# Mixer scan phase: weights split by a rounding load and an adding load, and high-half matmuls ahead of low-half ones

## The chip, the cores and the metric

The kernel runs on one core of one Trainium2 chip. The metric is the device time of one execution in microseconds (us); lower is better. A difference under about 0.2% cannot be told from none.

## What is computed

The reference is a stack of two blocks over 512 tokens of width 1024, batch 1, all in 32-bit floats. The first block has two layers, each a mixer and a feed-forward part; the second has one layer with another mixer and a two-matrix MLP. The change concerns the mixer of the first block:

```python
def _mixer(h, w_in, ...):
    p = h @ w_in                                  # 1024 x 6672
    (qkv, z, beta_r, a_r, hq, hf_fwd, hf_bwd, hi, hgate, gate_dn, gate_hg) = _split(p, IN_SIZES)
    ...                                           # 5-tap depthwise conv, silu, norms
    o_f = _gated_delta_rule(q, k, v, beta[0], g[0])          # 4 heads of 128, forward
    o_b = _flip(_gated_delta_rule(_flip(q), ...))            # and backward
    ...
    o_hf = _hgrn2_scan(qh, outs[0][0], ih, outs[0][1])       # 4 heads of 128, both directions
    ...
    merged = (jax.nn.sigmoid(gate_dn) * (o_dn @ w_branch_dn)
              + jax.nn.sigmoid(gate_hg) * (o_hg @ w_branch_hg))
    return merged @ w_out
```

## The kernel before

**Big products.** Every product with a weight matrix goes through `gemm` (line 264). A weight tile is 128 output columns by 8 blocks of 128 rows, 512 KB. `weights` (line 235) loads it from HBM into `wr` on SP's queue (line 244, three buffers), ScalarE (ACT) copies it to `wh`, rounded to the matmul's reduced 32-bit format fp32r (line 245, two buffers), and VectorE (DVE) subtracts, `wl = wr - wh`, which is what the rounding left over (line 246, two buffers). The moving operand is split the same way into `xh` and `xl`. For each of the 8 blocks `mm3` queues three matmuls into one PSUM bank `pd`: `wh` by `xh`, `wh` by `xl`, `wl` by `xh`, 24 for a tile, all recorded at line 257 (line 259 in a paced stretch).

**The scan phase of a mixer** runs twice, once for each layer, in the order of the string `ORDER`: four heads of the gated delta rule (`gdn_front`, `gdn_inverse`, `gdn_scan`) and four of the second scan (`hg_head`). It needs 37 weight tiles: a small one (`w_ba`, 16 columns) and 36 of 512 KB (nine for each head number: Q, K, V, Z of the first scan and two gates, query, input and output gate of the second). Beside these run chains of small steps: matmuls of 128x128 blocks, with DVE, ACT and GpSimd (POOL) working in turn between them. In `gdn_front`, `raw` (line 449) takes a product out of PSUM and DVE's line 454 makes the 5-tap convolution; `er` and `gb` are gate rows fetched by DMA; in `hg_head` each of seven steps has a copy `kc` on ACT (line 680), four matmuls (line 682), `att` and `qk` on DVE (lines 684, 686) and `pq` mostly on POOL (line 687).

**Order.** Each engine works through its own list in order, and an instruction that waits holds what is behind it. The lists are made when the program is built, by a scheduler that places instructions by priority and its own timing of them; the high-priority parts are those of the delta rule's chain. Weight loads are alone on SP's queue. POOL's queue before the change holds its elementwise steps and, outside the scan phases, eight small DMAs.

After a scan phase come gates, branch products and the output product, then the feed-forward part: long runs of weight tiles.

Of the kernel before, what the change touches and what calls it, by code (L numbers as in the profile page):

```python
# [173 lines left out]
class Net:  # L174
    def __init__(self, tc, I, O, at, ctx):
# [11 lines left out]
        self.n = 0  # L187
        self.pace, self.paced = [], 0
# [46 lines left out]
    def weights(self, src, lo="v", small=None):  # L235
        nc = self.nc
        n, c = src.shape[1], src.shape[2]
        pl, k, bf = (self.wp, 8, (3, 2, 2)) if small is None else (small, 2, (2, 2, 2))
        raw, hi, lw = (pl.tile([P, k, P], dt, name=self.nmx(t), tag=t, bufs=b) for t, dt, b in zip(("wr", "wh", "wl"), (F32, F32R, F32R), bf))
        if c == P:  # L240
            raw, hi, lw = raw[:, :n], hi[:, :n], lw[:, :n]
        else:
            raw, hi, lw = (t.rearrange("p a b -> p (a b)")[:, :n * c].rearrange("p (a b) -> p a b", b=c) for t in (raw, hi, lw))
        nc.sync.dma_start(raw, src)
        nc.scalar.activation(hi, raw, AF.Copy)  # L245
        (nc.vector if lo == "v" else nc.gpsimd).tensor_tensor(lw, raw, hi.bitcast(F32), op=ALU.subtract)  # L246
        return hi, lw
# [6 lines left out]
    def mm(self, *a, **k):  # L254
        """a matmul; those of a paced stretch are queued behind the steps of a scan, a few after each"""
# [8 lines left out]
    def gemm(self, srcs, xs, lo="v", m=P):  # L264
        bank = self.bank("pd")
        ps = bank[:m]
        nk = sum(s.shape[1] for s in srcs)
        k = 0
        for s in srcs:
            hi, lw = self.weights(s, lo)  # L270
            for i in range(s.shape[1]):
                self.mm3(ps, hi[:, i], lw[:, i], xs[k][0], xs[k][1], k == 0, k == nk - 1)
                k += 1
# [53 lines left out]
    def norm2_end(self, st):  # L327
        """the final norm of the first block and the first of the second in one"""
# [68 lines left out]
    def gdn_small(self, l, xs, rb, sp):  # L397
        """token-major gates of all heads: columns (c, d*4+h)"""
# [79 lines left out]
    def pair(t, width, b, first, off, n):  # L478
        """columns off .. off + n of a tile [P, 2 * width], blocks of b taken in turn from its halves, from half `first` at the start"""
# [238 lines left out]
    def mixer(self, l, state):  # L718
        nc, tc = self.nc, self.tc
        xs, rb = state  # L720
        with tc.tile_pool(name=f"sp{l}", bufs=1) as sp, tc.tile_pool(name=f"gt{l}", bufs=2) as gt:
            with tc.tile_pool(name=f"gi{l}", bufs=1) as self.gi, tc.tile_pool(name=f"gp{l}", bufs=1) as gp:
                with tc.high_priority():
# [6 lines left out]
                for u in ORDER.split():  # L730
# [8 lines left out]
                    else:  # L739
                        dn[h] = self.gdn_scan(l, h, xs, rb, sm, gp, sp, fr[h], zf[h])  # L740
                W = self.I[f"w_in{l}"]
# [478 lines left out]
```

## Time and profile before

| | |
|---|---|
| time, median of 3 runs | 2744.57 us (2740.33 to 2746.9) |
| span of the profiled execution, first to last instruction | 2742.3 us |
| TensorE (PE) busy | 2645.3 us, 96% |
| DVE busy | 1556.6 us, 57% |
| ACT busy | 1124.7 us, 41% |
| POOL busy | 329.2 us, 12% |

The page of the profile gives the span of its execution; which of the three times belongs to it is not listed, and between the span and the median lie 2.3 us. Busy time of PE is counted from modelled ends of matmuls, so it overlaps; idle time of PE and the clock that it was granted are the more useful columns.

### The profile page before, as it was taken

The page shows a single profiled execution, that of the slowest core. Times are in us where ns is not written, and L with a number is a line of the kernel's source. Part 1 is how long each engine was busy: PE and PEld are TensorE (multiplying, and loading weights), DVE is VectorE, ACT ScalarE, POOL GpSimd, SP SyncE. Part 2 cuts the span into 40 slices and gives each one's busy share as a digit, 9 for nine tenths or more (in the row PEclk, how much of TensorE's full clock was granted, in tenths as well). Part 3 has the DMA queues.
Part 4 walks back from the last instruction along what each step waited for, and adds up shares of the span by engine and source line. Part 5 has one row for each costly group of instructions (what it writes and reads, how often), then busy time and mean ns, then how long its engine had stood idle before and what let it go on. Part 6 is the DMA issues. An engine that isn't in the chain of part 4 may idle for free.

```text
span 2742.3 us, 32455 instructions
## 1 busy us (share of the span) xinstructions
PE 2645.3 (96%) x12674; PEld 2178.6 (79%) x12674; DVE 1556.6 (57%) x2234; ACT 1124.7 (41%) x1511; POOL 329.2 (12%) x282
## 2 busy tenths in 40 slices
PE   7999899999999979998999999999999999999999
PEld 4788788878888857887888788888777788888887
DVE  6778764455554366778644555534874444553442
ACT  6545544343333255455443433333446443332221
POOL 1112320001110011122200011100100111000000
PEclk9999989999999999999999999999999999999999
DMA  4112212253223332111123423234411232433332
GB/s 149 62 49 67 62 39 68 88 167 100 94 98 114 121 89 70 55 61 54 39 76 101 160 95 100 93 121 127 145 64 51 82 96 94 140 129 99 94 104 88
DMA packets 99064, 254.13 MB, mean 93 GB/s; under 512 B 10016, under 2 KB 31520, under 8 KB 98656
## 3 DMA queue, kind: packets, MB, share of 16 engines
q1 hardware_dynamic: 66960, 215.17, 24.5%
q10 hardware_dynamic: 31568, 35.85, 4.5%
q8 instruction: 100, 1.64, 0.2%
q0 software_dynamic: 384, 1.05, 0.1%
q14 instruction: 52, 0.43, 0.1%
HBM read 238.36 MB, written 12.62 MB: 92 GB/s over the span
## 4 chain that ended last, share of the span: by engine, by line
PE 49%; ACT 1%; DVE 0%; issue 0%; POOL 0%; ACTq 0%; DVEq 0%; POOLq 0%
PE pd L257 45%; PE ph L1065 1%; PE pl L1053 1%; PE pd L259 1%; ACT wh L245 0%; PE pr L1061 0%; ACT L1179 0%; PE pl L972 0%; PE ph L682 0%; PE pl L843 0%; DVE wl L246 0%; ACT rb L294 0%; ACT rb L295 0%; PE pl L1015 0%; PE ph L1039 0%
## 5 line engine op out<-in xcount | busy, mean ns | idle before, releaser
L257 PE MATMUL pd<-xh,wh 128*128 128x512 f32 (+1 forms) x3186 | 1265.8, 398 | 36.3 <-DVE raw L449 14.3
L257 PE MATMUL pd<-xh,wl 128*128 128x512 f32 (+1 forms) x3188 | 1258.0, 395 | 2.6 <-DVE wl L246 2.3
L257 PE MATMUL pd<-xl,wh 128*128 128x512 f32 (+1 forms) x3186 | 1253.7, 394 | 2.1 <-DVE xl L290 2.0
L245 ACT ACTIVATE wh<-wr 128x1024 fp32r<-128x1024 f32 (+5 forms) x449 | 434.9, 969 | 1011.3 <-PE pd L257 866.8
L257 PEld LDWEIGHTS pd<-xh,wh 128*128 128x128 f32 (+1 forms) x3186 | 600.2, 188 | 178.8 <-issue 20.9
L257 PEld LDWEIGHTS pd<-xl,wh 128*128 128x128 f32 (+1 forms) x3186 | 600.3, 188 | 139.2 <-issue 7.2
L257 PEld LDWEIGHTS pd<-xh,wl 128*128 128x128 f32 (+1 forms) x3188 | 600.0, 188 | 138.7 <-DVE wl L246 5.0
L246 DVE TENSOR_TENSOR wl<-wr,wh 128x1024 fp32r<-128x1024 f32 (+5 forms) x449 | 521.7, 1162 | 250.3 <-ACT wh L245 244.1
L1179 ACT ACT_TABLE_LOAD x116 | 148.8, 1283 | 8.7 <-issue 4.4
L394 DVE TENSOR_TENSOR g<-pd,rb 128x512 f32<-128x512 f32 x64 | 44.3, 692 | 158.2 <-PE pd L257 148.1
L803 POOL TENSOR_TENSOR fs<-fs,rb 128x512 f32<-128x512 f32 x44 | 56.9, 1294 | 506.3 <-ACT fs L802 506.3
L682 PE MATMUL ph<-pq,kc 128*128 128x128 f32 x448 | 74.8, 313 | 19.6 <-POOL er L569 6.7
L797 DVE TENSOR_TENSOR fg<-pd,rb 128x512 f32<-128x512 f32 x44 | 30.5, 693 | 109.9 <-PE pd L257 107.0
L682 PEld LDWEIGHTS ph<-pq,kc 128*128 128x128 f32 x448 | 66.7, 213 | 26.4 <-issue 19.2
L687 POOL TENSOR_TENSOR pq<-pq,f 128x512 f32<-128x512 f32 x48 | 58.8, 1225 | 230.7 <-PE ph L682 211.5
L805 DVE TENSOR_TENSOR fs<-fs,pd 128x512 f32<-128x512 f32 x44 | 30.3, 688 | 90.0 <-POOL fs L803 90.0
L801 DVE SCALAR_TENSOR_TENSOR fs<-fg,cv,fs 128x512 f32<-128x512 f32 x88 | 65.9, 749 | 3.6 <-ACT fs L799 1.9
L802 ACT ACTIVATE fs<-fs 128x512 f32<-128x512 f32 x44 | 27.8, 632 | 85.5 <-DVE fs L801 85.5
L394 DVE TENSOR_TENSOR mh<-pd,rb 128x512 f32<-128x512 f32 x32 | 22.1, 692 | 70.2 <-PE pd L257 68.8
L680 ACT COPY kc<-qk 128x512 f32<-128x512 f32 x56 | 36.9, 659 | 52.2 <-PE ph L682 44.5
L454 DVE SCALAR_TENSOR_TENSOR qk<-raw,cv,qk 128x512 f32<-128x512 f32 x64 | 54.1, 858 | 2.6 <-ACT qk L452 2.2
L684 DVE COPY_PREDICATED att<-um,ph 128x512 f32<-128x512 uint8 x56 | 41.2, 736 | 21.5 <-PE ph L682 21.2
(332 smaller groups left out, 2442.5 us busy)
## 6 DMA issues: line engine op xcount, KB each, us to landing
wr<-in_w_in_dram SPq DMA_DIRECT2D x126, 512.0 KB, 3.3
wr<-in_w_up_dram SPq DMA_DIRECT2D x88, 512.0 KB, 3.3
wr<-in_w_m_dram SPq DMA_DIRECT2D x64, 512.0 KB, 3.8
wr<-in_w_dn_dram SPq DMA_DIRECT2D x32, 512.0 KB, 3.6
wr<-in_w_gt_dram SPq DMA_DIRECT2D x32, 512.0 KB, 3.3
wr<-in_w_out_dram SPq DMA_DIRECT2D x24, 512.0 KB, 3.4
xd<-xn ACTq DMA_DIRECT2D x40, 256.0 KB, 2.0
xo<-xd ACTq DMA_DIRECT2D x32, 256.0 KB, 2.8
```

Source lines behind the costliest of these rows:

```text
L245: nc.scalar.activation(hi, raw, AF.Copy)
L246: (nc.vector if lo == "v" else nc.gpsimd).tensor_tensor(lw, raw, hi.bitcast(F32), op=ALU.subtract)
L257: return self.nc.tensor.matmul(*a, **k)
L394: self.nc.vector.tensor_tensor(out, ps, rb, op=ALU.mult)
L454: V.scalar_tensor_tensor(o, raw[:, j:j + T], self.col(f"dnc{l}_{j}", ch), o, op0=ALU.mult, op1=ALU.add)
L680: A.copy(kc.rearrange("p (n e b) -> p n e b", e=2, b=hh), self.pair(qk, T, hh, 0, 0, T))
L682: PE.matmul(pl[:, c], kc[:, c * P:(c + 1) * P], self.pair(pq, T, hh, 1, c * P, P), start=True, stop=True)
L684: V.copy_predicated(att, self.um[:, o:o + P].unsqueeze(1).to_broadcast([P, 4, P]), pl)
L687: (G if hh > 1 else V).tensor_tensor(halves(pq, hh, True), halves(pq, hh, True), tot(F, n, 0, n + 1, hh), op=ALU.mult)
L801: nc.vector.scalar_tensor_tensor(g, gp[:, j:j + T], self.col(f"fc{l}_{j}", m), g, op0=ALU.mult, op1=ALU.add)
L803: nc.gpsimd.tensor_tensor(g, g, rb, op=ALU.mult)
L1179: nc.scalar.preload_act_table_set(s)
```

## The change

Of a weight tile in a scan phase, POOL's queue now issues a load from HBM straight into `wh`, which rounds on the way (line 248); ACT writes `-wh` into `wl` (line 249); and POOL's queue issues a second load of the same block that adds what it reads to `wl` (line 250). `wr`, SP's load and DVE's subtraction fall away for these tiles. Elsewhere they stay as they were. In every tile, `gemm` now queues the 16 matmuls with `wh` first and then the 8 with `wl`.

```diff
-    def weights(self, src, lo="v", small=None):
+    def weights(self, src, small=None):
...
+        dma = self.dma_lo and small is None
...
-        nc.sync.dma_start(raw, src)
-        nc.scalar.activation(hi, raw, AF.Copy)
-        (nc.vector if lo == "v" else nc.gpsimd).tensor_tensor(lw, raw, hi.bitcast(F32), op=ALU.subtract)
+        if dma:
+            nc.gpsimd.dma_start(hi, src)
+            nc.scalar.activation(lw, hi.bitcast(F32), AF.Copy, scale=-1.0)
+            nc.gpsimd.dma_start(lw, src, accum_op=ALU.add)
+        else:
+            nc.sync.dma_start(raw, src)
+            nc.scalar.activation(hi, raw, AF.Copy)
+            nc.vector.tensor_tensor(lw, raw, hi.bitcast(F32), op=ALU.subtract)
         return hi, lw
...
-        for s in srcs:
-            hi, lw = self.weights(s, lo)
-            for i in range(s.shape[1]):
-                self.mm3(ps, hi[:, i], lw[:, i], xs[k][0], xs[k][1], k == 0, k == nk - 1)
-                k += 1
+        for j, s in enumerate(srcs):
+            hi, lw = self.weights(s)
+            n = s.shape[1]
+            for i in range(n):
+                self.mm(ps, hi[:, i], xs[k + i][0], start=j == 0 and i == 0, stop=False)
+                self.mm(ps, hi[:, i], xs[k + i][1], start=False, stop=False)
+            for i in range(n):
+                self.mm(ps, lw[:, i], xs[k + i][0], start=False, stop=j == len(srcs) - 1 and i == n - 1)
+            k += n
...
                 with tc.tile_pool(name=f"gi{l}", bufs=1) as self.gi, tc.tile_pool(name=f"gp{l}", bufs=1) as gp:
+                self.dma_lo = True
...
+                self.dma_lo = False
                 W = self.I[f"w_in{l}"]
```

The scheduler then orders everything anew, and line numbers behind `weights` move by 8 to 13. Three places show what that does.

PE at the start of the first layer's scan, before: the tile `pd_333` with its weights `wh_335` and `wl_336`, in the pattern that it keeps for all 24 matmuls.

```order
L257 MATMUL pd_333<-xh_111,wh_335 128x512
L257 MATMUL pd_333<-xl_112,wh_335 128x512
L257 MATMUL pd_333<-xh_111,wl_336 128x512
L257 MATMUL pd_333<-xh_116,wh_335 128x512
L257 MATMUL pd_333<-xl_117,wh_335 128x512
L257 MATMUL pd_333<-xh_116,wl_336 128x512
```

PE at the same place now: the end of the high half of the second tile (`pd_368`), and behind it the low half of the first (`pd_331`).

```order
L265 MATMUL pd_368<-xh_151,wh_369 128x512
L265 MATMUL pd_368<-xl_152,wh_369 128x512
L265 MATMUL pd_368<-xh_158,wh_369 128x512
L265 MATMUL pd_368<-xl_159,wh_369 128x512
L265 MATMUL pd_331<-xh_111,wl_333 128x512
L265 MATMUL pd_331<-xh_116,wl_333 128x512
L265 MATMUL pd_331<-xh_123,wl_333 128x512
L265 MATMUL pd_331<-xh_130,wl_333 128x512
```

Both tiles' high halves (32 matmuls) now stand ahead of the first matmul that needs a `wl`; later tiles mostly have their 16 and their 8 one behind the other.

POOL in the first `hg_head` of the first layer, before: the steps `pq` follow each other with nothing between.

```order
L687 TENSOR_TENSOR pq_768<-pq_768,f_159_923 128x2x128x2
L687 TENSOR_TENSOR pq_768<-pq_768,f_766 128x2x64x4
L687 TENSOR_TENSOR pq_768<-pq_768,f_159_923 128x2x32x8
L687 TENSOR_TENSOR pq_768<-pq_768,f_766 128x2x16x16
L687 TENSOR_TENSOR pq_768<-pq_768,f_159_923 128x2x8x32
```

POOL at the same steps now.

```order
L698 TENSOR_TENSOR pq_761<-pq_761,f_148_912 128x2x128x2
L250 DMA wl_1461<-in_w_in_dram 128x1024
L698 TENSOR_TENSOR pq_761<-pq_761,f_759 128x2x64x4
L248 DMA wh_1526<-in_w_in_dram 128x1024
L250 DMA wl_1527<-in_w_in_dram 128x1024
L698 TENSOR_TENSOR pq_761<-pq_761,f_148_912 128x2x32x8
L248 DMA wh_1557<-in_w_in_dram 128x1024
L250 DMA wl_1558<-in_w_in_dram 128x1024
L698 TENSOR_TENSOR pq_761<-pq_761,f_759 128x2x16x16
L248 DMA wh_1594<-in_w_in_dram 128x1024
L698 TENSOR_TENSOR pq_761<-pq_761,f_148_912 128x2x8x32
```

Between the steps stand the loads of later tiles: `wh` (rounding, which waits for PE to have used the buffer's tile before) and `wl` (adding, which waits for ACT's `-wh`, and that for the rounding load of the same tile).

DVE while the second head's front runs in the first layer, before.

```order
L454 SCALAR_TENSOR_TENSOR qk_112_621<-raw_284,cv,qk_112_621 128x512
L454 SCALAR_TENSOR_TENSOR qk_112_621<-raw_285,cv,qk_112_621 128x512
L454 SCALAR_TENSOR_TENSOR qk_112_621<-raw_284,cv,qk_112_621 128x512
L449 TENSOR_TENSOR raw_285<-pd_702,rb_168 128x512
L508 SCALAR_TENSOR_TENSOR bn_451<-pl_435,gb_292 128x1024
L246 TENSOR_TENSOR wl_804<-wr_802,wh_803 128x1024
L454 SCALAR_TENSOR_TENSOR qk_112_621<-raw_284,cv,qk_112_621 128x512
L521 TENSOR_TENSOR gb_292<-gb_292,pl_463 128x1024
```

DVE at the same place now.

```order
L465 SCALAR_TENSOR_TENSOR qk_108_617<-raw_284,cv,qk_108_617 128x512 x2
L465 SCALAR_TENSOR_TENSOR qk_108_617<-raw_283,cv,qk_108_617 128x512
L465 SCALAR_TENSOR_TENSOR qk_108_617<-raw_284,cv,qk_108_617 128x512
L465 SCALAR_TENSOR_TENSOR qk_108_617<-raw_283,cv,qk_108_617 128x512
L465 SCALAR_TENSOR_TENSOR qk_108_617<-raw_284,cv,qk_108_617 128x512
L465 SCALAR_TENSOR_TENSOR qk_108_617<-raw_283,cv,qk_108_617 128x512 x2
L519 SCALAR_TENSOR_TENSOR bn_447<-pl_431,gb_291 128x1024
L532 TENSOR_TENSOR gb_291<-gb_291,pl_459 128x1024
L460 TENSOR_TENSOR raw_284<-pd_696,rb_168 128x512
```

The subtraction at line 246 is gone from between the convolution's steps; the other instructions keep their kinds, in a slightly different order.

## Rows read from the trace of the kernel before

**Rows 1.** Busy time by stretch: both scan phases, and 100 us of feed-forward work.

```profile
core 0: us, PE busy (x) PEld busy (x) DVE busy (x) ACT busy (x) POOL busy (x), PEclk, DMA share, GB/s
24.00:445.00 421.00, 385.20 (x2152) 329.42 (x2152) 302.27 (x482) 219.35 (x294) 90.11 (x67) 0.95 0.19 58
940.00:1430.00 490.00, 449.83 (x2446) 380.04 (x2445) 329.75 (x516) 238.64 (x321) 93.61 (x73) 0.95 0.21 64
...
700.00:800.00 100.00, 100.00 (x443) 82.81 (x442) 53.17 (x64) 37.82 (x47) 12.94 (x10) 1.00 0.30 98
```

**Rows 2.** PE's waits in 24:450, then in 1000:1450: total us, times, longest.

```profile
PE ph L698 <- DVE att L684: 4.4, 2, 3.4
PE pd L257 <- DVE zsh L394: 4.2, 1, 4.2
PE pd L257 <- DVE raw L449: 3.9, 1, 3.9
...
PE ph L682 <- DVE att L684: 3.0, 1, 3.0
...
PE pd L257 <- DVE raw L449: 10.4, 1, 10.4
PE pd L257 <- DVE zsh L394: 5.1, 1, 5.1
PE ph L698 <- DVE att L684: 4.8, 2, 3.4
...
PE pd L257 <- DVE wl L246: 2.0, 1, 2.0
```

**Rows 3.** DVE's costliest group by line in 24:445: busy us, mean ns.

```profile
L246 DVE TENSOR_TENSOR wl<-wr,wh 128x1024 fp32r<-128x1024 f32 x39 | 50.1, 1284 | 8.3 <-ACT wh L245 8.2
```

**Rows 4.** Subtractions in the timeline: start us, duration us.

```profile
54.90 1.23 DVE L246 TENSOR_TENSOR wl<-wr,wh 128x1024 fp32r<-128x1024 f32 x1 [0.16 <-ACT wh L245]
...
388.08 1.21 DVE L246 TENSOR_TENSOR wl<-wr,wh 128x1024 fp32r<-128x1024 f32 x1
...
1011.94 1.21 DVE L246 TENSOR_TENSOR wl<-wr,wh 128x1024 fp32r<-128x1024 f32 x1
...
1013.68 1.21 DVE L246 TENSOR_TENSOR wl<-wr,wh 128x1024 fp32r<-128x1024 f32 x1
...
1052.36 3.40 DVE L246 TENSOR_TENSOR wl<-wr,wh 128x1024 fp32r<-128x1024 f32 x1
```

**Rows 5.** Matmuls of one tile in the timeline, PE.

```profile
18.48 0.39 PE L257 MATMUL pd<-xh,wh 128*128 128x512 f32 x1
...
18.71 0.40 PE L257 MATMUL pd<-xl,wh 128*128 128x512 f32 x1
...
18.94 0.39 PE L257 MATMUL pd<-xh,wl 128*128 128x512 f32 x1
...
19.17 0.40 PE L257 MATMUL pd<-xh,wh 128*128 128x512 f32 x1
```

**Rows 6.** DMA issues: engine, KB each, median us to landing; POOL's time for one, ns.

```profile
wr<-in_w_in_dram SPq DMA_DIRECT2D x126, 512.0 KB, 3.3
...
cw<-in_cw_dram ACTq DMA_DIRECT2D x2, 1024.0 KB, 5.4
...
k<-tn POOLq DMA_DIRECT2D x4, 128.0 KB, 2.9
...
L961 POOL DMA_DIRECT2D k<-tn x4: 518/518/687, 1953.3 to 1963.8; - x4
```

**Rows 7.** ACT's rounding copy, all tiles: ns minimum, median, maximum.

```profile
L245 ACT ACTIVATE wh<-wr x449: 284/1061/1068, 3.1 to 2727.2; 128x1024 fp32r<-128x1024 f32 x121, 128x512 fp32r<-128x512 f32 x10, 128x256 fp32r<-128x256 f32 x10, 128x768 fp32r<-128x768 f32 x8
```

**Rows 8.** Matmuls with `wl` alone, by stretch: us, PE busy (count), clock, DMA.

```profile
24.00:100.00 76.00, 28.99 (x71) 0.91 0.28 77
```

**Rows 9.** DMA in the first 24 us, 40 slices of 0.6 us; SP's first loads of `w_in`.

```profile
GB/s 0 0 6 140 368 279 340 411 392 376 234 170 121 297 390 410 403 403 399 420 410 434 403 437 423 321 191 27 0 0 0 61 177 423 212 164 348 321 27 14
...
9.19 0.85 SPq L244 DMA_DIRECT2D wr<-in_w_in_dram  x2
```

**Rows 10.** POOL by line in 24:445: busy us, mean ns, idle before and its releasers.

```profile
L687 POOL TENSOR_TENSOR pq<-pq,f 128x512 f32<-128x512 f32 x24 | 29.3, 1219 | 115.4 <-PE ph L682 108.0 <-issue 7.3
```

More of the change, by code (lines that the diff above doesn't have):

```diff
@@ L238, in weights @@
         pl, k, bf = (self.wp, 8, (3, 2, 2)) if small is None else (small, 2, (2, 2, 2))
-        raw, hi, lw = (pl.tile([P, k, P], dt, name=self.nmx(t), tag=t, bufs=b) for t, dt, b in zip(("wr", "wh", "wl"), (F32, F32R, F32R), bf))
+        dma = self.dma_lo and small is None
+        raw, hi, lw = (None if dma and t == "wr" else pl.tile([P, k, P], dt, name=self.nmx(t), tag=t, bufs=b) for t, dt, b in zip(("wr", "wh", "wl"), (F32, F32R, F32R), bf))
         if c == P:
-            raw, hi, lw = raw[:, :n], hi[:, :n], lw[:, :n]
+            raw, hi, lw = (t if t is None else t[:, :n] for t in (raw, hi, lw))
         else:
-            raw, hi, lw = (t.rearrange("p a b -> p (a b)")[:, :n * c].rearrange("p (a b) -> p a b", b=c) for t in (raw, hi, lw))
-        nc.sync.dma_start(raw, src)
-        nc.scalar.activation(hi, raw, AF.Copy)
-        (nc.vector if lo == "v" else nc.gpsimd).tensor_tensor(lw, raw, hi.bitcast(F32), op=ALU.subtract)
+            raw, hi, lw = (t if t is None else t.rearrange("p a b -> p (a b)")[:, :n * c].rearrange("p (a b) -> p a b", b=c) for t in (raw, hi, lw))
+        if dma:
[6 more added lines that the diff above has]
+            nc.vector.tensor_tensor(lw, raw, hi.bitcast(F32), op=ALU.subtract)
         return hi, lw
@@ L262, in mm, with gemm @@
             self.pace.pop(0)
-    def gemm(self, srcs, xs, lo="v", m=P):
+    def gemm(self, srcs, xs, m=P):
         bank = self.bank("pd")
         ps = bank[:m]
-        nk = sum(s.shape[1] for s in srcs)
         k = 0
-        for s in srcs:
-            hi, lw = self.weights(s, lo)
-            for i in range(s.shape[1]):
-                self.mm3(ps, hi[:, i], lw[:, i], xs[k][0], xs[k][1], k == 0, k == nk - 1)
-                k += 1
+        for j, s in enumerate(srcs):
[7 more added lines that the diff above has]
+            k += n
         return bank
@@ L740, in mixer @@
                         dn[h] = self.gdn_scan(l, h, xs, rb, sm, gp, sp, fr[h], zf[h])
+                self.dma_lo = False
                 W = self.I[f"w_in{l}"]
```

## The prediction

> **What bounds the kernel now.** I read three views in this order: busy time by stretch, then PE's waits, then the timeline at the longest of them. In a feed-forward stretch PE is busy for 100 of 100 us [rows 1]. There a faster DVE buys nothing. The two scan phases are another matter: PE is idle for 421.0 - 385.2 = 35.8 us of the first stretch and 490.0 - 449.8 = 40.2 us of the second, 76 us together, and its granted clock there averages 0.95 instead of 1.00 [rows 1]. The clock loss is (385.2 + 449.8) x 0.05 = 42 us more, since the clock falls to its lower level (1.2 GHz) after PE has idled for some us. So the room for any change of the scan phases is 76 + 42 = 118 us, 4.3%, and each microsecond of wait costs about 42 / 76 = 0.55 us of slow clock on top, a factor of 1.55.
>
> Who ends the waits? The nine largest that DVE ends make 4.4 + 4.2 + 3.9 + 3.0 in the first phase and 10.4 + 5.1 + 4.8 + 3.0 (the row `att` at L682 stands again with the same number) + 2.0 in the second: 40.8 us [rows 2]. DVE is busy for 302.3 of 421 us there, the most after PE [rows 1], and the subtraction of the weights is its costliest line, 50.1 us or 17% of its work [rows 3]. So there is something to gain; the question is whether the subtraction stands in the queue where PE waits, and what the new route of the weights costs.
>
> **What is removed.** 74 subtractions leave DVE (37 tiles in each of two layers, two of them small). I looked for them in DVE's queue just ahead of the long waits. One at 54.90 stands ahead of the `raw` that ends the 3.9 us wait; two, at 1011.94 and 1013.68, stand ahead of the `raw` that ends the 10.4 us wait; one at 388.08 stands ahead of the `att` that ends the 3.0 us wait, with a twin in the second layer; and the one at 1052.36, stretched to 3.40 us, is itself waited for, 2.0 us [rows 2, 4]. That is 5 x 1.21 + 2.0 = 8.0 us that I expect to see go. The other 40.8 - 8.0 = 32.8 us of these waits have no subtraction right before them; I let them shrink with DVE's load, by 17%: 5.4 us. Together 13.4 us, with the clock 13.4 x 1.55 = 20.8 us. The bounds: nothing, if what is late next (the gate rows by DMA, `gb`, POOL's steps) takes its place at once, and 40.8 x 1.55 = 63 us if all nine waits go.
>
> 74 loads leave SP's queue, which has nothing else to do there, so that is worth nothing by itself. What hid them was a buffer more (`wr`) and a queue of their own.
>
> **What is added.** ACT's copy of 1.06 us [rows 7] becomes a copy of the same size with a factor; I cost it at no difference. POOL issues 148 loads. The nearest row is a POOL issue of 0.52 us for half the partitions [rows 6]; at 0.5 to 1.0 us each that is 74 to 148 us on an engine busy for 90 + 94 of 911 us [rows 1]. It is covered by POOL's idle time, 115 us before the `pq` steps of one phase alone [rows 10]; in-order waiting is the danger, not the sum.
>
> The path of a tile gets longer. Before, `wr` was there early. Now, with two buffers of `wh`, tile i's rounding load can start when the high half of tile i-2 is done, and then follow: the load, ACT's copy, the adding load, and only then the low half of tile i. I price the rounding load as a 512 KB load, 3.3 us from issue to landing, and the adding load, which reads source and target, as a 1024 KB load, 5.4 us [rows 6]; a 128 KB load that POOL issued landed in 2.9 us, so its route shows no penalty by itself [rows 6]. One POOL step of 1.22 us in front of an issue [rows 10] goes on top. The chain is 3.3 + 1.06 + 5.4 + 1.22 = 11.0 us.
>
> Against it stands PE's own work between the same two points. Matmuls start every 0.23 us, whichever of the three pairs follows which [rows 5], so a high half is 16 x 0.23 = 3.68 us and a low half 1.84. Between the end of the high half of i-2 and the start of the low half of i lie a low, a high, a low and a high half: 11.04 us. So where tile follows tile with nothing between, the chain is just covered; a further microsecond is not. For a longer chain L three tiles take L + 5.52 us, so a tile takes (L + 5.52) / 3. With one ACT operation of 1.06 us queued in front as well, L is 12.0, a tile 5.84 instead of 5.52, 0.32 us more. Tiles stand so densely only at the start of each phase: 71 / 8 = 9 tiles in the first 76 us [rows 8], 18 in both layers; later PE has the scan's small matmuls between. 18 x 0.32 x 1.55 = 9 us; I take half, 4.5 us, since not every issue finds something ahead of it. The bounds: none, with the adding load at 3.3 us; and with both loads at twice their rows, L = 6.6 + 1.06 + 10.8 + 1.22 = 19.7, a tile 8.4 us, 18 x 2.9 x 1.55 = 81 us.
>
> The start pays a little. The first weights now come while the activations do; before, SP issued them behind, at 9.19 us, and the DMA engines move about 400 GB/s in these us [rows 9]. 512 KB more ahead of `x` is 524 KB / 400 GB/s = 1.3 us.
>
> **What is moved.** High half first changes nothing in the pitch [rows 5], and in the other 375 tiles PE hardly waits [rows 1], so I cost it at zero; in the scan phases it is what makes the cover of 11 us possible: in the old order the second matmul but one would already need the low half.
>
> **The sum.** -20.8 + 4.5 + 1.3 = -15.0 us. The span of 2742.3 becomes 2727.3, and with the 2.3 us by which the median of the runs stands above the span, **2730 us**, 0.5% faster. Its own range, with the gain halved or doubled and the dense tiles free or at 9 us, is 2710 to 2740.
>
> **The rivals.**
> *The adding load lands late (slower).* Nothing in the trace shows an adding load; its price is mine. The gain is used up (20.8 - 1.3 = 19.5 us) when a dense tile loses 19.5 / (18 x 1.55) = 0.70 us, that is at L = 13.1, an adding load that lands 7.6 us after its issue. At 9 us L is 14.6 and a tile takes 6.7, so 18 x 1.2 x 1.55 = 33 us: 2744.6 - 19.5 + 33 = 2758. At the upper bound it is 2806. For it speaks that ACT and POOL wait in order; against it, that 5.4 us for the double amount is a measured row.
>
> *POOL's queue holds the scan's steps (slower).* In the list of POOL a step `pq` now often stands behind an adding load, which waits for ACT, which waits for a rounding load just issued: 3.3 + 1.06 = 4.4 us. Mostly a tile's 5.5 us of matmuls stand in PE's list between two steps and cover it. If half of some 40 such steps come 1 us late at PE, 20 x 1.55 = 31 us: 2761. POOL's `pq` now waits for PE and not the other way round [rows 10], which speaks against it.
>
> *DVE holds POOL's issues (slower).* DVE and POOL hold each other up in this trace: the subtraction at 1052.36 took 3.40 instead of 1.21 us [rows 4], while POOL was at work. If each issue is held by that 2.2 us, L is 11.0 + 4.4 = 15.4, a tile 7.0, and 18 x 1.45 x 1.55 = 40 us make 2765. The Trainium skill ("SBUF — State Buffer", the box on DVE blocking DMA) says that POOL's cores cannot write the descriptors of a DMA while certain DVE operations hold the port that they share, and advises the queues of ACT or SP. By that rule this change moves 74 loads the wrong way; no row here shows a held issue, and POOL's eight issues took 0.52 to 0.69 us [rows 6].
>
> *Nothing moves (same).* Five subtractions go, and the same waits end in the next late thing: within 2739 to 2750, say 2743.
>
> *More goes than I count (faster).* All nine waits: 2744.6 - 63 = 2681.
>
> **How the numbers follow.** My forecast gets 0.40, the better case 0.10, no change 0.15, the late adding load 0.20, POOL's queue 0.09, DVE on POOL 0.06. A difference under 0.2% (5.5 us) cannot be told from none by this measurement. That makes 0.50 faster, 0.15 the same, 0.35 slower. The range 2690 to 2785 holds all but the ends of the better case and of the late load, about 0.1 together with what I have not thought of on either side.
>
> **What would show it.** Right: in the scan phases DVE's busy time falls by some 45 us each, the 10.4 us wait shrinks by 2 to 3, the adding load lands in 4 to 7 us, and PE's waits for `wl` stay under 5 us in all. Wrong: PE waits for `wl` or `wh` in tens of us, the adding load lands after 7.6 us, `ph` at the step matmuls waits for POOL, or ACT's time before the negated copy grows while `kc` stands behind it. A changed order from the scheduler, with other matmuls late than now, would upset the list of waits above without any of these.

## The result and the profile after

The change made the kernel slower: 2779.36 us median of four runs (2773.09 to 2780.32) against 2742.45 us (2738.83 to 2746.9), a ratio of 1.0131 with a 95% interval of 1.0114 to 1.0148. I had forecast 2730.

In the profiled execution the span grew by 2777.1 - 2742.3 = 34.8 us. PE's idle time grew by 117.9 - 97.0 = 20.9 us and its busy time, for the same 12674 matmuls, by 13.9 us: the mean granted clock was 0.980 of full speed instead of 0.983. The same two stretches as in [rows 1], now after the change (us, busy time of each engine with its count of instructions, granted clock, DMA share, GB/s):

```profile
core 0: us, PE busy (x) PEld busy (x) DVE busy (x) ACT busy (x) POOL busy (x), PEclk, DMA share, GB/s
24.00:445.00 421.00, 375.62 (x2079) 315.79 (x2078) 263.38 (x441) 210.43 (x284) 134.20 (x134) 0.94 0.44 101
940.00:1430.00 490.00, 442.80 (x2387) 372.19 (x2385) 279.79 (x465) 229.56 (x309) 139.27 (x145) 0.95 0.43 101
```

DVE gave up 302.3 - 263.4 = 38.9 us and 50.0 us, as forecast. The DMA engines are twice as busy. PE did less in the same time. PE's waits show why; first those of 24:450, then of 1000:1450 (total us, times, longest), as in [rows 2]:

```profile
PE pf L310 <- ACT raw L471: 11.2, 3, 5.9
PE pf L310 <- ACT raw L473: 6.2, 1, 6.2
PE ph L693 <- ACT kc L691: 5.8, 2, 4.7
PE ph L693 <- POOL pq L698: 4.4, 6, 1.7
PE pd L265 <- DVE raw L460: 3.8, 1, 3.8
PE pd L265 <- DMA wl<-in_w_in_dram: 2.4, 4, 1.1
PE ph L693 <- DVE att L695: 1.9, 1, 1.9
...
PE pf L310 <- ACT raw L473: 8.2, 1, 8.2
PE ph L693 <- POOL pq L698: 7.1, 5, 2.9
PE pd L265 <- DMA wl<-in_w_in_dram: 5.9, 6, 1.8
PE ph L693 <- ACT kc L691: 5.7, 2, 4.0
PE pf L310 <- ACT raw L471: 5.3, 2, 3.3
PE pl L510 <- DVE qk L478: 2.7, 1, 2.7
```

Over both windows, all the waits that DVE ended fell from 52.0 us (40.8 of them in the nine rows of [rows 2]) to 19.3, of which the three here make 3.8 + 1.9 + 2.7 = 8.4 us. What stands at the top now is ACT, with `raw` and `kc`: 11.2 + 6.2 + 5.8 + 8.2 + 5.7 + 5.3 = 42.4 us. Before, PE never waited for `kc`, and for ACT's `raw` 10.2 us:

```profile
PE pf L299 <- ACT raw L460: 6.2, 2, 4.6
...
PE pf L299 <- ACT raw L460: 4.0, 1, 4.0
```

PE waits for `wl` itself 8.3 us. So the tile's path is late at PE only in part; something on it holds ACT. ACT's group of the negated copy in 24:445 (busy us, mean ns of one; idle time just before it and what ended that), and two rows of POOL in the same stretch, the second of which answers to [rows 10]:

```profile
L249 ACT ACTIVATE wl<-wh 128x1024 fp32r<-128x1024 f32 x35 | 37.0, 1056 | 92.9 <-DMA wh<-in_w_in_dram 54.8 <-issue 16.5 <-PE pd L265 9.4
L250 POOL DMA_DIRECT2D wl<-in_w_in_dram x35 | 30.3, 865 | 151.6 <-ACT wl L249 122.3 <-ACT w L603 7.3 <-DVE v L557 5.9
L698 POOL TENSOR_TENSOR pq<-pq,f 128x512 f32<-128x512 f32 x24 | 31.2, 1300 | 19.0 <-issue 10.1 <-PE ph L693 8.9
```

ACT stands idle for 92.9 us before 35 copies, over half of it for the rounding load; the rounding copy of the kernel before had 45.1 us of idle time in front of it there, 40.6 of them for PE. One such place in the timeline (start, duration, idle time before in brackets), POOL, ACT and PE in turn:

```profile
159.03 0.89 POOL L248 DMA_DIRECT2D wh<-in_w_in_dram  x1
...
164.91 1.06 ACT L249 ACTIVATE wl<-wh 128x1024 fp32r<-128x1024 f32 x1 [7.26 <-DMA wh<-in_w_in_dram]
165.87 0.60 ACT L691 COPY kc<-qk 128x512 f32<-128x512 f32 x1
...
166.57 2.05 PE L693 MATMUL ph<-pq,kc 128*128 128x128 f32 x8 [4.71 <-ACT kc L691]
```

The load is issued at 159.03, and the copy starts 5.9 us later, when it has landed. The copy waits for it and `kc`, a step of the scan that needs nothing of that tile, stands behind the copy in ACT's list. PE needs `kc`, not the weights, and waits 4.71 us; the 2.05 us for eight small matmuls, which took 1.16 us at 159.45, are the lower clock after it: the granted clock is 1.00 in 150:160 and 0.51, the level of 1.2 GHz, in 166:169.

The page's rows of the new loads (KB each, median us from issue to landing), where [rows 6] has 3.3 us for SP's load:

```profile
wh<-in_w_in_dram POOLq DMA_DIRECT2D x72, 512.0 KB, 5.0
wl<-in_w_in_dram POOLq DMA_DIRECT2D x72, 512.0 KB, 5.4
```

My price of the adding load was right, that of the rounding load was 1.7 us short. It was slow behind an adding load: the 26 rounding loads that were issued less than 1 us behind one have a median of 6.2 us, the 36 that were issued more than 2 us behind one 3.7. In run g1 below, which has no adding loads, the median of all is 3.6. The Trainium skill ("DMA: Bandwidth & Descriptors", on the anatomy of a DMA of the gpsimd path) fits one such DMA by 2.0 us plus its bytes over 436 GB/s, by which 512 KB would be an estimated 3.2 us; g1's 3.6 us is near that, the trace of the changed kernel does not agree, its medians are 5.0 and 5.4 us.

### The profile page after: what moved, and what is told of

It reads as the page before. It is cut to its first block, busy times and chain, and to the rows that moved or that the text cites. A ratio compares the mean times of both kernels' runs of the same rounds, so it can differ in the third digit from the quotient of the medians.

```text
span 2777.1 us, 32476 instructions
## 1 busy us (share of the span) xinstructions
PE 2659.2 (96%) x12674; PEld 2183.7 (79%) x12674; DVE 1457.5 (52%) x2160; ACT 1126.1 (41%) x1511; POOL 438.0 (16%) x430
## 3 DMA queue, kind: packets, MB, share of 16 engines
q0 software_dynamic: 21696, 76.82, 12.4%
## 4 chain that ended last, share of the span: by engine, by line
PE 81%; DMA 5%; issue 4%; ACT 4%; DVE 4%; POOL 2%; ACTq 0%; POOLq 0%; SPq 0%; DVEq 0%
PE pd L265 70%; DMA wh<-in_w_in_dram 2%; PE pd L267 1%; DMA er<-gd 1%; PE ph L693 1%; ACT L1192 1%; DVE qk L465 1%; PE pl L1066 1%; PE ph L1078 1%; DMA wl<-in_w_in_dram 1%; DVE qk L697 0%; PE pr L618 0%; ACT wl L249 0%; PE pr L608 0%; PE ph L714 0%
## 5 line engine op out<-in xcount | busy, mean ns | idle before, releaser
L265 PE MATMUL pd<-xh,wh 128*128 128x512 f32 (+2 forms) x3184 | 1262.3, 397 | 21.3 <-ACT xh L300 9.5
L265 PE MATMUL pd<-xl,wh 128*128 128x512 f32 (+2 forms) x3184 | 1256.5, 395 | 0.7 <-DVE xl L301 0.7
L265 PE MATMUL pd<-xh,wl 128*128 128x512 f32 (+1 forms) x3192 | 832.6, 396 | 8.5 <-DMA wl<-in_w_in_dram 8.3
L265 PEld LDWEIGHTS pd<-xh,wh 128*128 128x128 f32 (+2 forms) x3184 | 601.0, 189 | 165.3 <-ACT xh L300 10.0
L265 PEld LDWEIGHTS pd<-xl,wh 128*128 128x128 f32 (+2 forms) x3184 | 600.5, 189 | 135.9 <-issue 7.3
L253 ACT ACTIVATE wh<-wr 128x1024 fp32r<-128x1024 f32 (+2 forms) x375 | 358.0, 955 | 574.5 <-PE pd L265 486.3
L254 DVE TENSOR_TENSOR wl<-wr,wh 128x1024 fp32r<-128x1024 f32 (+2 forms) x375 | 415.2, 1107 | 267.1 <-PE pd L265 153.1
L249 ACT ACTIVATE wl<-wh 128x1024 fp32r<-128x1024 f32 (+1 forms) x74 | 76.6, 1035 | 200.8 <-DMA wh<-in_w_in_dram 115.9
L250 POOL DMA_DIRECT2D wl<-in_w_in_dram x72 | 62.3, 865 | 303.4 <-ACT wl L249 241.1
L697 DVE TENSOR_TENSOR qk<-qk,f 128x512 f32<-128x512 f32 x56 | 62.0, 1107 | 26.6 <-ACT kc L691 23.7
```

The source lines that it names most:

```text
L249: nc.scalar.activation(lw, hi.bitcast(F32), AF.Copy, scale=-1.0)
L250: nc.gpsimd.dma_start(lw, src, accum_op=ALU.add)
L254: nc.vector.tensor_tensor(lw, raw, hi.bitcast(F32), op=ALU.subtract)
L265: return self.nc.tensor.matmul(*a, **k)
L697: V.tensor_tensor(halves(qk, hh, False), halves(qk, hh, False), tot(F, n, 1, n - 1, hh), op=ALU.mult)
```

## The experiments

Theory H (ACT held): the copy waits in ACT's list for a rounding load that can't start earlier, since there are two buffers of `wh`, and what stands behind it comes late. Its rivals: O, the order of matmuls costs by itself; P, POOL's list and the late adding load. S came up on the way: the order costs through the engines' lists, which the scheduler builds from when it thinks a buffer is free.

The table has all runs. "Against before" is the ratio of the times with its 95% interval. The three columns behind it are differences to the span of before in the profiled execution, by part: up to the start of PE's 4283rd matmul in order of time (between the phases, at 922 us before), from there to its 7715th (behind the second, at 1640 us), and the rest. They are of one execution each; that of e8 was 4 us slower than the run's median, that of f2 4 us faster.

| run | median us | against before | first phase | second | rest |
|---|---|---|---|---|---|
| the change | 2779.36 | 1.0131 (1.0114 to 1.0148) | +13.8 | +13.3 | +7.7 |
| e1 order alone | 2770.26 | 1.0101 (1.0083 to 1.0119) | +10.6 | +9.0 | +3.6 |
| e2 change, third wh | 2743.49 | 1.0004 (0.9994 to 1.0014) | -3.6 | -4.1 | +7.0 |
| e3 copy on DVE | 2784.45 | 1.0147 (1.0128 to 1.0165) | +16.7 | +15.1 | +8.1 |
| e4 adding load alone | 2750.56 | 1.0028 (1.0016 to 1.004) | +2.3 | -2.4 | +6.7 |
| e5 loads, old order | 2802.32 | 1.0217 (1.0197 to 1.0237) | +21.9 | +31.3 | +5.3 |
| e6 order, third wh | 2771.26 | 1.0108 (1.009 to 1.0127) | +13.2 | +7.5 | +6.6 |
| e7 before, third wh | 2763.74 | 1.0084 (1.0068 to 1.01) | +13.2 | +4.5 | +1.7 |
| e8 before, loads twice | 2767.39 | 1.0094 (1.0072 to 1.0116) | +20.9 | +2.5 | +4.1 |
| e9 order, last block as before | 2751.36 | 1.0037 (1.0024 to 1.005) | +5.7 | -2.3 | +6.8 |
| e10 change, third wl | 2769.64 | 1.0099 (1.0082 to 1.0116) | +7.8 | +11.2 | +8.7 |
| e11 loads for hg tiles, third wh | 2763.99 | 1.0084 (1.0069 to 1.0099) | +5.2 | +5.1 | +8.0 |
| e12 e2 with e9's order | 2743.67 | 1.001 (0.9999 to 1.002) | -0.3 | -1.1 | +0.2 |
| f1 change, pq on DVE | 2775.5 | 1.0118 (1.0103 to 1.0133) | +12.8 | +13.5 | +5.4 |
| f2 e2, pq on DVE | 2747.88 | 1.0024 (1.0014 to 1.0034) | -3.4 | -3.8 | +6.7 |
| f3 before, no subtraction | 2728.86 | 0.9945 (0.993 to 0.996) | -8.0 | -8.8 | +1.1 |
| g1 e2, no adding load | 2737.8 | 0.998 (0.997 to 0.9989) | -6.9 | -4.9 | +5.0 |
| g2 e2, 4 KB adding load | 2740.47 | 0.9992 (0.9981 to 1.0003) | -6.5 | -5.0 | +7.4 |

### The order, the buffer, the copy and the adding load, one at a time

**e1, the order alone.**

```diff
-                self.dma_lo = True
+                self.dma_lo = False
```

> Only the order of matmuls of the change: every weight tile by one load of SP, ACT's copy and DVE's subtraction as before, high halves first. Theory H (ACT held: the negated copy waits in ACT's list for the rounding load, and raw and kc behind it come late) and theory P (POOL's list and the adding load are late) expect no change, 2737 to 2748 us. Theory O (the order itself costs, since a tile now wants its xh and xl every 0.46 us instead of every 0.69 us, and the scheduler places everything else by it) expects 2755 us or more, with PE's waits for xh and xl as the sign.

27 us slower, with nothing of the new route in it: O or something like it, against H and P as I had put them. But PE's waits for `xh` and `xl` are not the sign; the longest wait is for a bank that DVE's `raw` frees. PE, and what ACT did some 20 us before:

```profile
45.33 1.06 ACT L253 ACTIVATE wh<-wr 128x1024 fp32r<-128x1024 f32 x1 [1.44 <-PE pd L265]
46.81 0.96 ACTq L577 DMA_DIRECT2D er<-gd  x2
...
67.51 0.79 PE L265 MATMUL pd<-xh,wh 128*128 128x512 f32 x1 [12.16 <-DVE raw L460]
```

The loads of the gate rows went out at 43.28 us in the kernel before and go out at 46.81 here; they feed DVE's `gb`, behind which `raw` stands. A rounding copy that waits for PE now stands ahead of them in ACT's list, but it had ended at 46.39. What they waited for is the store `gd` that they read from: it was issued at 43.61 us instead of 41.82 and landed after 3.2 us instead of 1.4. Before, the same halt took 4.6 + 3.9 us.

**e2, a third buffer of wh in the changed kernel.**

```diff
-... (self.wp, 8, (3, 2, 2)) if small is None ...
+... (self.wp, 8, (3, 3, 2)) if small is None ...
```

> The changed kernel with three buffers of wh instead of two, so that a rounding load may start a tile (5.5 us) sooner. Theory H: ACT's idle time before the negated copy for the load, 54.8 us in the first phase, falls below 25 us, and 20 of the 37 us come back, 2752 to 2765 us. Theory P: POOL still waits 132 us for ACT and pq behind it, the adding loads are not sooner than the copies, 2770 to 2782 us. Theory O: 2779 us, nothing changes.

All of the loss came back, more than H had said. ACT's group in 24:445:

```profile
L249 ACT ACTIVATE wl<-wh 128x1024 fp32r<-128x1024 f32 x34 | 35.9, 1056 | 36.3 <-PE pd L265 35.1 <-DMA wh<-in_w_in_dram 1.2
```

The wait for the load is 1.2 us instead of 54.8, that for `kc` at PE 0.4 instead of 5.8. POOL still issues both loads of each tile. In the two phases together PE stands idle for 80.8 us instead of 103.1: of the 22.3 us, 10.4 are waits for `kc`, 6.5 for `wl` and 4.8 for POOL's `pq`. ACT's `raw` hardly changes, 28.4 us instead of 30.9, so these waits are not what the third buffer gave back. By parts, e2 is 7.7 us faster than the kernel before in the two phases and loses 7.0 us behind them.

What the third buffer changed is seen in POOL's list. I counted it in the trace: in the changed kernel 65 of the 71 rounding loads behind the first stand behind the adding load of the tile just before. That adding load waits for ACT's copy of its tile, and the copy for the rounding load of its tile. So the tiles are filled one after the other, with 8.2 to 8.5 us from rounding load to rounding load in this place, where PE's work for a tile is 5.5:

```profile
116.38 0.86 POOL L250 DMA_DIRECT2D wl<-in_w_in_dram  x1 [4.62 <-ACT wl L249]
116.93 0.86 POOL L248 DMA_DIRECT2D wh<-in_w_in_dram  x1
124.82 0.85 POOL L250 DMA_DIRECT2D wl<-in_w_in_dram  x1 [7.03 <-ACT wl L249]
125.38 0.86 POOL L248 DMA_DIRECT2D wh<-in_w_in_dram  x1
133.07 0.87 POOL L250 DMA_DIRECT2D wl<-in_w_in_dram  x1 [6.83 <-ACT wl L249]
133.62 0.87 POOL L248 DMA_DIRECT2D wh<-in_w_in_dram  x1
```

In e2 one of 71 does; the loads run a tile ahead, and now wait for PE alone:

```profile
111.75 0.85 POOL L250 DMA_DIRECT2D wl<-in_w_in_dram  x1 [2.62 <-ACT wl L249]
115.41 0.56 POOL L248 DMA_DIRECT2D wh<-in_w_in_dram  x1 [2.81 <-PE pd L265]
```

So H has the wait right and its reason only in part. Of the 127.9 us that ACT waits for rounding loads in all of the changed kernel, 95.5 are for loads that POOL issued right behind another instruction of its list, with no wait for PE left, and 32.3 for loads that PE had just released. No run keeps two buffers with the rounding load ahead of the adding load, so list and buffer are not told apart.

**e3, the copy on DVE.**

```diff
-            nc.scalar.activation(lw, hi.bitcast(F32), AF.Copy, scale=-1.0)
+            nc.vector.tensor_scalar(lw, hi.bitcast(F32), -1.0, None, op0=ALU.mult)
```

> The changed kernel with the negated copy on DVE instead of ACT; loads and order stay. Theory H: PE's waits that ACT's raw and kc end (about 37 us in both phases) fall under 15 us, and waits that DVE ends grow instead, since the wait for the rounding load now stands in DVE's list; the sum is open, 2765 to 2800 us. Theory P: the waits of PE for raw and kc stay above 30 us, since they were not made by the copy, 2775 to 2785 us.

PE's waits for `kc` are gone, and DVE now does what ACT did, with its own steps behind it. The first row is DVE's, the others are PE's, all in 24:450:

```profile
DVE wl L249 <- DMA wh<-in_w_in_dram: 37.0, 13, 6.3
...
PE pf L310 <- ACT raw L471: 11.3, 3, 4.3
PE pf L310 <- ACT raw L473: 6.1, 1, 6.1
PE pd L265 <- DVE zsd L405: 5.6, 2, 2.8
PE pl L560 <- DVE v L557: 4.2, 2, 4.0
```

But the waits for `raw` stayed, 17.4 us in each phase, so H was wrong about them: they are not made by ACT's copy. The longest of them in the first phase, 6.2 us in the change and 6.1 in e3, stand at the halt at the gate rows.

**e4, the adding load alone.**

```diff
-            nc.gpsimd.dma_start(hi, src)
+            nc.sync.dma_start(raw, src)
+            nc.scalar.activation(hi, raw, AF.Copy)
```

> The changed kernel without the rounding load: SP loads wr as before and ACT rounds it to wh, ACT then writes the negated copy to wl, and POOL's adding load stays. ACT gets 74 copies of 1.06 us more, 78 us, and waits for no load of POOL. Theory H: nearly all comes back, 2740 to 2756 us. Theory P: the adding load behind ACT, and pq behind the adding load, stay, so 2768 us or more. Theory O: 2775 us or more.

As H expects: 29 of 37 us back without POOL's rounding load, though ACT copies 74 tiles more. It takes the load out of POOL's list as well.

**e5, the new loads in the old order.**

> Only the new route of the weights in the scan phases (rounding load, negated copy, adding load), with the old order high, high, low of each block. If the order is what costs and the route is nearly free (the order alone made 2770, both together 2779), 2745 to 2755 us. Theory H, in the form that the chain of a tile is longer than what covers it: in the old order wh comes free at the end of tile i-2 and wl is wanted at the start of tile i, so one tile of 5.5 us covers a chain of 11 us, two dense tiles take 16.5 us instead of 11, and 18 dense tiles alone lose some 50 us: 2800 us or more.

The old order wants `wl` at its third matmul and gives `wh` back at the tile's end. In all of the span:

```profile
PE pd L265 <- DMA wl<-in_w_in_dram: 51.3, 30, 4.8
```

That is the chain of 11 us against a cover of one tile. So the order is needed by the route, as the prediction has it, although it costs when it is alone.

### Is it the buffer, or the lists?

**e6, e7, e10: a third buffer elsewhere**: of `wh` with the order alone, of `wh` in the kernel before, of `wl` in the changed one (each by the three numbers in e2's diff: 3, 3, 2 in the first two and 3, 2, 3 in the third).

> The order alone (old route of the weights), with three buffers of wh. Theory H in a wider form: in the order alone ACT stood idle 62.7 us before its rounding copies in the first phase (45.1 in the kernel before), since a copy waits in ACT's list until PE gives a wh back, and the gate rows' loads, which ACT issues, and kc stand behind it. Then a third buffer takes most of the 27 us back: 2740 to 2752 us and ACT's idle time there under 45 us. If the order costs by what PE wants next (xh, xl, evacuations), nothing changes: 2765 to 2775 us.

> The kernel before with three buffers of wh and nothing else. If the third buffer is worth something by itself, whatever the change, 2715 to 2735 us, and what the third buffer gave the changed kernel was no repair of the change. If it only repairs what the change made late, 2738 to 2748 us.

> The changed kernel with a third buffer of wl instead of wh, as a control for the run with the third wh (2743 us). Theory H (the rounding load can't be issued before wh of tile i-2 is given back, and ACT waits for it with raw and kc behind): wl was never what a load waited for, so 2772 to 2786 us, with ACT's idle time before the negated copy as in the changed kernel, some 93 us in the first phase. If a buffer more of any kind helps, or another list of the scheduler did it, 2740 to 2765 us.

e6 refutes the wider form of H: the buffer does nothing for the order alone. e7 surprised me most: the kernel before loses 21 us by one more buffer. e10 gives back 10 of 37 us, a little more than H allowed; ACT's idle time before the copy stays, 85.5 us, 79.9 of it for the load, and so does POOL's list (67 of 71 rounding loads behind the adding load before). PE's waits for `kc` fall all the same, from 11.5 to 2.5 us, so ACT's idle time by itself is no measure of the loss. A buffer is no gain in itself. In the changed kernel it is that of `wh` that counts, and with it goes the wait for the rounding load.

What e1, e6 and e7 share is seen in PE's list. Ahead of the steps of the second scan (four matmuls of `ph` each) stand tile matmuls that cover the wait for the step before. Their number, counted in PE's list of the first layer for two steps at a time (eight matmuls), ahead of such pairs 6 to 10, which the texts below call steps:

```
before                    24  44 148  45   3
order alone (e1, e6)       6  19 194  42   9
before, third wh (e7)      5  15 177  24   0
the change                37  36 114  44  28
change, third wh (e2)     38  30 119  39  33
order, last block (e9)    24  44 148  45   3
```

Single step by single step, ahead of steps 9 to 14 (the second head), these are 24, 0, 24, 24, 20 and 4 in the kernel before, 18, 6, 0, 0, 19 and 15 in e1, 19, 5, 0, 0, 15 and 17 in e7. I read this so: a `wh` that comes free earlier lets the scheduler put tiles earlier, and then there are none where a step waits. In e7 PE goes from the scan's small matmuls at 212.26 to the next step with nothing between:

```profile
212.26 0.61 PE L538 MATMUL pl<-zc,v 128*128 128x128 f32 x4
221.12 1.19 PE L682 MATMUL ph<-pq,kc 128*128 128x128 f32 x4 [8.25 <-DVE att L684]
```

The change and e2 have nearly the same list of PE in this layer, and 17 us between them in the first phase: there it is not PE's list, but POOL's has changed.

**e9, the last block as before.** The high halves of seven blocks, the low halves of seven, then high, high, low of the last, so that `wh` comes free where it did:

```diff
-            for i in range(n):
+            for i in range(n - 1):
...
+            self.mm3(ps, hi[:, n - 1], lw[:, n - 1], xs[k + n - 1][0], xs[k + n - 1][1], ...)
```

> The order alone (old route of the weights), but the two high-half matmuls of the last block and its low-half matmul stand at the end of the tile, as before; the first 14 high-half matmuls still come first. wh so comes free at the end of the tile, as in the kernel before. In PE's list the tile matmuls then stand between the steps of the scan just as before (24, 44, 148, 45 and 3 of them ahead of steps 6 to 10), where the order alone put 6, 19, 194, 42 and 9. Theory S (the order cost 27 us only through the list that the scheduler made of the earlier release of wh, with too few tile matmuls ahead of some steps): 2738 to 2750 us. If high halves first cost by themselves (xh and xl wanted faster, wl used late), 2762 to 2775 us.

19 of 27 us come back, 1 us above S's range. 14 of 16 high halves still come first, so theory O can hold at most for the 8 to 10 us that are left. Of these, 6.8 us lie behind the phases.

**e12 and e11**: the change with third `wh` and e9's order; the new route for the tiles of `hg_head` alone, with third `wh`.

> The changed kernel with three buffers of wh and with the last block's three matmuls at the end of the tile. Its list (27, 40, 164, 26 and 10 tile matmuls ahead of steps 6 to 10) is near that of before, its rounding loads have the time that the third buffer gives less 1.8 us. Theory H with S: ACT waits little for the rounding load and the list is good: 2728 to 2743 us. If the gain of the third buffer was a lucky list, 2755 us or more.

> The new route only for the 40 tiles of the heads whose scan runs step by step (20 in each layer), the old route for the others, which stand dense at the start; three buffers of wh. Theory H: no rounding load is late, half of the subtractions leave DVE, and the gate rows meet no second load: 2725 to 2743 us. If only half of the tiles on the new route brings half of its cost and gain, it stays within 2740 to 2750 us. If theory S holds for it, the list (24, 45, 142, 33 and 20 tile matmuls ahead of steps 6 to 10, near that of before) gives no loss.

e12 repeats e2's time with another list (27, 40, 164, 26, 10), 0.7 us above its range; so e2 was not one lucky list. POOL's list is as in e2 (one of 71). e11 failed all three theories: PE's list is near that of before, and yet PE waits 12.4 and 12.9 us at the gate rows for DVE's `raw`. The five numbers don't describe that place.

### Bytes, POOL's list, and what the subtraction was worth

**e8, the bytes alone**: in the kernel before, SP loads each block once more into a spare buffer.

```diff
+        if self.twice and small is None:
+            nc.sync.dma_start(self.wp.tile([P, n * c], F32, ..., tag="wx", bufs=1), ...)
```

> The kernel before, with each weight block of the scan phases loaded a second time by SP into a spare buffer that nobody reads, behind the load that is used: as many bytes as in the changed kernel, with no new wait on ACT, DVE or POOL. If the bytes themselves cost (the gate rows gb and er land later: in the changed kernel at its first phase 10.0 us instead of 7.7 us), 2750 to 2762 us, with the sum of PE's waits in the first 60 us after the gate rows 5 us or more longer in each phase. If not, 2740 to 2747 us.

It did something else than I meant. All 72 loads ran between 10 and 276 us, as nobody reads them. At the 900th matmul (200 us in the kernel before) it was 3.9 us late, at the 1000th (225 us) 20.4. Between them ACT's own DMA issues waited for SP's loads:

```profile
213.84 0.60 ACT L626 ACTIVATE sqd<-pr 128x512 f32<-128x512 f32 x1 [4.95 <-DMA wx<-in_w_in_dram]
...
222.27 1.28 ACT L1184 ACT_TABLE_LOAD   x1 [7.83 <-DMA wr<-in_w_in_dram]
```

So it adds a wait on ACT after all and doesn't decide the question of bytes beyond the first 200 us.

**f1, f2: all steps pq on DVE**, in the changed kernel and in e2's.

```diff
-            (G if hh > 1 else V).tensor_tensor(halves(pq, hh, True), ...)
+            V.tensor_tensor(halves(pq, hh, True), ...)
```

> The changed kernel (two buffers of wh) with all steps pq on DVE, so that none stands in POOL's list behind an adding load. Theory P (POOL's list): PE's waits for pq of POOL (4.4 and 7.1 us in the two phases) go, and with the clock some 15 us or more of the 37 come back: 2750 to 2765 us. Theory H: ACT still waits for the rounding loads, 80 us or more in the first phase, and 2768 us or more stays.

> The changed kernel with three buffers of wh and all steps pq on DVE: DVE takes 48 steps of 0.7 us (34 us) of the 100 us that the subtractions left. If POOL's pq is what is late next (3.6 and 3.1 us of waits with the third wh), 2730 to 2738 us. If the gate rows and the list decide, 2740 to 2755 us.

The steps `pq` in POOL's list are worth 4 us at most (2779.4 to 2775.5), and nothing with the third buffer (2743.5 to 2747.9). So P is out as I had put it. ACT's idle time before the copy in the first phase fell to 77.3 us, 40.3 of it for the loads, which is under H's 80. The adding loads stay ahead of the rounding loads in f1 (65 of 71 as in the change), so f1 says nothing against that part of POOL's list.

**f3, no subtraction; g1, g2, no or a small adding load.**

```diff
+        if self.bare and small is None:
+            return hi, hi
```
```diff
-            nc.gpsimd.dma_start(lw, src, accum_op=ALU.add)
+            nc.gpsimd.dma_start(lw[:1], src[:1], accum_op=ALU.add)
```

> The kernel before with the subtraction of the weights left out in the scan phases and nothing in its place: the low-half matmuls read the high half instead, so that part of the computation is left out; matmuls, loads and ACT's copies stay. It measures the term of the prediction by itself: 74 subtractions less on DVE. The prediction's step: 20.8 us less, 2721 us (2700 to 2735). Theory N: what is late next (gate rows, ACT's steps) takes the place of the subtractions at once, 2738 to 2750 us.

> The changed kernel with three buffers of wh and without the adding loads: wl stays the negated copy of wh, so that part of the computation is left out. The rounding load, ACT's copy and the matmuls stay, and in the first phase the list has the same tile matmuls ahead of steps 6 to 10 as with the adding loads (38, 30, 119, 39, 33). If the adding loads (bytes, POOL's place for them, the late wl) take back the 13 us that leaving out the subtraction gave the kernel before, 2726 to 2734 us; if it is the list, the rounding loads or ACT, 2739 to 2746 us.

> As g1, but the adding load stays for one of the 128 partitions (4 KB instead of 512 KB); the other partitions keep the negated copy, so that part of the computation is left out. POOL issues it at the same place and waits for ACT's copy as before; the bytes are gone. Against the kernel with the third wh and whole adding loads (2743.5 us): if the bytes cost, as g1; if POOL's waiting issue or the wait for wl cost, 2739 us or more while g1 is faster.

f3 frees DVE of the same work as the change does (262.5 us busy in 24:445) and adds nothing: 13.2 us faster, inside the range of the prediction's step and 8 us short of its number. PE's list is new there too (33, 33 and 121 tile matmuls ahead of pairs 6 to 8, where the kernel before has 24, 44 and 148), so the 13.2 us are the removal with what the scheduler made of it.

g1 (2737.8 us) lies between its two ranges, and g2 (2740.5 us) is 2.7 us above g1, where a cost of POOL's issue or of the wait for `wl` was expected and not one of the bytes; but g2's runs spread from 2733.9 to 2750.3 us. Against e2, g2 gains 3.0 us and g1 5.7; the intervals of e2 and g2 overlap. In the profiled executions g1 and g2 gain some 3 us more than e2 in the first phase (-6.9 and -6.5 against -3.6, f3 -8.0) and 1 us in the second. The loads of `er` in 38:75 landed after 8.4 us in e2 and 5.7 in g2. So the adding load's bytes cost a few us at most, and how many is not shown.

## Why the prediction was wrong

**What bounds the kernel** held: 27.1 of the 34.8 us lie in the two phases, and 34.8 us of span for 20.9 us of idle time are a factor of 1.67 where I had 1.55. The other 7.7 us lie behind the phases, where I had expected nothing.

**What is removed** was over-sized. DVE's load fell as said, but the 20.8 us of gain measured 13.2 (f3, with a list of its own). The nine waits were not quite the largest: a wait of 2.8 us for DVE's `bt` is left out, and one of 2.0 is in.

**What is added** is where the prediction failed, in one sentence: "ACT's copy of 1.06 us [rows 7] becomes a copy of the same size with a factor; I cost it at no difference." The copy takes 1.06 us still. But it waits for another thing: before, 40.6 of ACT's 45.1 us of idle time in front of it were for PE to give a `wh` back; now 54.8 of 92.9 are for the rounding load. And that load was late for a reason that my chain left out. I had it start "when the high half of tile i-2 is done"; in 65 of 71 cases it stood in POOL's list behind the adding load of tile i-1, so that load, copy and adding load of one tile came before the load of the next, 8.2 us a tile in the rows under e2, where I had 5.84. I named in-order waiting on POOL as "the danger", and looked only at the `pq` steps. I didn't ask either what stands behind the copy in ACT's list. `kc` did, and the last part of the prediction named that sign without a price: PE waited for it 11.5 us, where it had not waited before. For `wl` it waited 8.3 us in all (12.9 us with the factor, where I had 4.5, and above the 5 us that I had set as a sign). That the late rounding load is what costs is shown by e2 (ACT's wait for the load 54.8 to 1.2 us, the time back to that of before) and e4; e10 shows that a buffer of another kind does not take it away. That POOL's list made it late is read from the traces of the change, e2, e10 and e12, and no run changes that list alone. The rounding load itself, priced 3.3 us, took 5.0. The start paid 10.3 - 8.9 = 1.4 us of PE's idle time in the first 24 us, where I had 1.3.

**What is moved** failed too: "so I cost it at zero". Alone it costs 27 us (e1), and, as I read e9, through the lists: e9 leaves the high halves first, releases `wh` where it was released before, and 19 us are gone. The two losses don't add (27 and 60 alone, 37 together). How the list of e1 turns into time is seen at one place only, the gate rows, and there a later store takes part; the rest is argued from the counts. Behind the phases, where I had the order at zero too, PE waits at two places of the second block. The rows are from 1600 us on, before and after:

```profile
PE pd L257 <- ACT wh L245: 3.3, 1, 3.3
PE pf L878 <- DVE gy L880: 1.4, 1, 1.4
...
PE pd L265 <- DVE tc L405: 6.6, 1, 6.6
PE pf L891 <- POOL gv L882: 3.0, 1, 3.0
```

The wait for `tc` is 3.8 us in e1 and 6.4 in e2, and the one for `gv` 3.0 in both, so they come without the new loads too. With a third `wh` and the old order (e7) the one for `tc` is 4.6.

**The rivals.** The late adding load was not it: it landed after 5.4 us, and leaving most of its bytes out of e2 gives 3 us. What the traces point to is its place in POOL's list, ahead of the next rounding load, which none of my rivals has. POOL's queue held `pq` (idle time before them for PE fell from 108.0 us [rows 10] to 8.9), but moving them away gives 4. DVE holding POOL's issues did not show: the 72 issues of the adding load took 0.844 to 0.883 us each, all alike, and those of the rounding load 0.532 to 1.106, with 0.86 where one follows an adding load at once (116.93 above) and 0.56 where it does not (e2, 115.41). What the Trainium skill says in "SBUF — State Buffer" (the box on DVE blocking DMA) would have shown as issues or landings stretched by DVE's work; no run here shows it, and the 1.7 us by which the rounding load was late are gone in g1 but for 0.3, though DVE works there as in e2.

**Still open.** Where the 13 us of f3 go in e2. In the phases e2 gains 7.7 us and f3 16.8; there PE waits 28.4 us for ACT's `raw` in e2 and 6.6 in f3. Behind them e2 loses 7.0 us, e1 3.6 and f3 1.1. Why e12 loses only 0.2 there and e9, with the same order, 6.8, is open, as is where the 27 us of the order go when the new loads and a third `wh` come with it. No version here beats the kernel before while it computes the whole: e2 and e12 equal it. A version with the new order in the scan phases alone was not run.

## What to carry to other kernels

When an instruction's input moves from a buffer that is filled early to a load that starts late, price the engine that waits in order for it: what stands behind it in its list, not only what is made of its result. Look at the list of the queue that issues the loads as well: where the second load of one tile stands ahead of the first load of the next, the tiles are filled one after the other. A buffer count is part of such a change; here the third `wh` put the loads a tile ahead, but the same buffer in the kernel before cost 21 us. Where a scheduler builds the lists, a change that frees a buffer earlier can cost: count what stands ahead of the waits before and after. That can be seen before anything runs, though e11 shows that it does not tell everything.

## What the runs showed that I had not expected

- One more buffer of `wh` made the kernel before 21 us slower (2763.7 against 2742.4) and the changed one 36 us faster.
- ACT stood idle for up to 7.83 us while its DMA issues waited for loads that SP had issued (e8), though the two share no buffer.
- The 512 KB loads that POOL issued landed after 5.0 us (rounding) and 5.4 us (adding, onto what is there), nearly alike, where SP's of the same matrix took 3.2 to 3.3 us. Without the adding loads (g1) the rounding loads took 3.6.
